# FFN first gemm of a transformer block: high and low activation halves as one 512-column operand, four products accumulating in one pair of banks

## Chip, cores and metric

The kernel runs on one core of one Trainium2 chip. The metric is the device time of one execution in microseconds, the median over several runs. A profile comes from one further execution under the hardware profiler.

## What is computed

One block: an attention and retention mixer with a residual, then a gated FFN with a residual, then a final norm. The change lies in the FFN and in the last lines of the final norm.

```python
S, D, D_FF = 512, 1024, 2816
hffn = modulate(rmsnorm(x, g_norm2[l]), shift2, scale2)
a, u = jnp.split(jnp.einsum('bsd,df->bsf', hffn, w_ffn_in[l]), 2, axis=-1)
x = x + gate2[:, None, :] * jnp.einsum('bsf,fd->bsd', jax.nn.silu(a) * u, w_ffn_out[l])
return rmsnorm(x, g_final)
```

Everything is float32.

## The kernel before

**Precision.** A float32 matmul is made of three matmuls in a faster 32-bit format (fp32r). Each operand is split into a high part, a rounded copy that ScalarE writes, and a low part, source minus high, that VectorE subtracts; high·high, high·low and low·high are accumulated. In names, whi and wlo are the two halves of a weight tile, and q, qp, v, s and h are pools whose tiles hold activations, weights or their halves.

**First gemm of the FFN.** The output columns of w_ffn_in are worked off in 11 pairs p (0 to 10): 256 columns of a and the 256 of u that belong to them. The tokens are two halves of 256 columns, and so is the contraction, two halves of 512 rows (four steps k of 128). The 2 × 2 × 2 block product is done with seven products instead of eight, on sums of blocks. The table SEVEN names the activation block of each: products 1 to 7 use A11, A12, S4, A22, S1, S2 and S3, where the S blocks are sums of the A blocks, made once. The weight blocks are summed for each pair on VectorE (`sums`, L1213). One product (`product`) is 2 column blocks of 128 × 4 steps k × 3 matmuls, each with 256 token columns: 24 matmuls into one PSUM bank, the two column blocks side by side in its 512 columns.

**What a product's result goes through** (`take_out`). Product 1 is copied out to p1; 2 goes on accumulating in the same bank and silu of the sum is s0; 6 is added to p1, giving u2; 5 is copied to c22; 7 is added to u2, and so on, until the pair's two results are split into high and low halves for the second gemm. Products 5, 6 and 7 each take a bank of the pool z, 1 and 4 one of the pool ps; 2 and 3 go on in the banks of 1 and 5.

**Second gemm.** Pairs are grouped in chunks (FF_CHUNKS: pair 0, then 1 and 2, 3 and 4, and so on). For each chunk there are four items ("out", c, i) of two output blocks each (`run_out`): 12 matmuls of 512 columns per block and 24 per item for a chunk of two pairs, half of that for chunk 0 with its one pair, then `residual` (L1158) on VectorE.

**Order.** The list `work` has all products and out items in the order in which they run; a pair's products go 1, 6, 5, 7, 2, 4, 3, with an out item after the third and the sixth. Weights are prepared AHEAD = 5 items ahead (`prepare_item`), and a scheduler then settles how the instructions of each engine are ordered. The FFN's opening, with all of pair 0 and parts of pairs 1 and 2, is written out by hand for PE, VectorE and ScalarE. Weight loads go out on SP's queue into the buffers raw (3) and araw (2). For products 1 and 2 the low half of the weights is not subtracted on VectorE: ScalarE writes the negative high half (L839), and a DMA of POOL's queue adds the raw weights to it (L840, `low_dma`). A pair's second such weight is named h<-raw in the trace, the first s<-raw.

**Tail.** The last blocks of the second gemm are done by halves of the tokens, squares are summed over the features by matmuls with ones, the roots taken (L1580 to L1584), and the rows multiplied and stored: `norm` (L1589, stores of `o`) for the first half of the tokens, `norm2` (L1603, stores of `fin`) for the second.

Of the kernel before, what the change touches and what calls it, by code (L numbers as in the profile page):

```python
# [19 lines left out]
P = 128  # L20
D = 1024
S = 512
# [93 lines left out]
def kernel(  # L116
# [1059 lines left out]
    def low7(key, src, tag):  # L1176
        hi, lo = acts7[key], quarter(tag)
        ins = nc.vector.tensor_sub(lo, src, f(hi))
        acts7[key] = tiles(hi), tiles(lo)
        return ins.ins  # L1180

# [67 lines left out]
    def product(p, n, o, first, last, at=None, then=None, late=None):  # L1249


        hi, lo = (tiles(t) for t in ready.pop((p, n)))
        ah, al = acts7[SEVEN[n]]
        early = ((hi, ah), (lo, ah)) if late == "a" else ((hi, ah), (hi, al))
        rest = (hi, al) if late == "a" else (lo, ah)
        for i in range(2):
            c = slice(i * P, (i + 1) * P)
            for k in range(4):
                if i * 4 + k == at:
                    then()  # L1260
                oc = o[:, i * 256 : (i + 1) * 256]
                a, z = first and i == 0 and k == 0, last and i == 1 and k == 3
                if late:
                    for n_, (w, x) in enumerate(early):
                        mm(oc, w[:, k, c], x[:, k, :], a and n_ == 0, False)
                else:
                    mm3(oc, hi[:, k, c], lo[:, k, c], ah[:, k, :], al[:, k, :], a, z)
        if late:
            w, x = rest
            for i in range(2):  # L1270
                c = slice(i * P, (i + 1) * P)
                for k in range(4):
                    ins = mm(o[:, i * 256 : (i + 1) * 256], w[:, k, c], x[:, k, :],
                             False, last and i == 1 and k == 3)
            return ins

    def run_product(p, n):

        d = part.setdefault(p, {})
        if n in (1, 4):  # L1280
            d["xy"[n > 1]] = ps()
        elif n in (5, 6, 7):
            d[" vzw"[n - 4]] = psz()
        product(p, n, d[" xxvyvzw"[n]], n not in (2, 3), n not in (1, 5))
        take_out(p, n)

    def take_out(p, n):
# [13 lines left out]
        elif n == 7:  # L1301
            d["u3"] = tmp()
            nc.vector.tensor_add(d["u3"], d["w"], d["u2"])
            nc.vector.tensor_add(d["c22"], d["c22"], d["u3"])
        elif n == 4:
            nc.vector.tensor_add(d["u3"], d["y"], d["u3"])
            nc.scalar.activation(d["u3"], d["u3"], AF.Silu)
        elif n == 3:
            tag = "h" if chunk_of[p] % 2 else "s"
            nc.vector.tensor_add(d["u2"], d["v"], d["u2"])  # L1310
            nc.vector.tensor_mul(d["u2"], d["u2"], d["s0"])
            nc.vector.tensor_mul(d["u3"], d["u3"], d["c22"])
            hi, lo = pair(tag), pair(tag)
            for hv, t in zip(HALVES, (d["u2"], d["u3"])):
                split(hi[:, :, hv], lo[:, :, hv], t.rearrange("p (a b) -> p a b", a=2))
            ff_acts[chunk_of[p]] += [(hi[:, i, :], lo[:, i, :]) for i in range(2)]
            del part[p]

# [70 lines left out]
    with tc.manual_schedule(engines={nc.vector.engine, nc.scalar.engine, nc.tensor.engine}):  # L1389
# [18 lines left out]
        for d in tail:  # L1408
# [16 lines left out]
        sq5 = square(5, h1)  # L1425
        high7("A11", m00, "v")
        scaled(m01, 1, range(2), h0, r0)
        add_square(sq5, h1)
        low7("A11", m00, "v")
# [4 lines left out]
        high7("A12", m01, "v")  # L1434
# [4 lines left out]
        a01, l01 = acts7["A12"], quarter("v")  # L1439
        nc.vector.tensor_sub(l01[:, 0:S], m01[:, 0:S], f(a01)[:, 0:S])  # L1440
        add_square(sq7, h1)
        acts7["A12"] = tiles(a01), tiles(l01)
        d0, d1 = part.setdefault(0, {}), part.setdefault(1, {})
# [6 lines left out]
        g1 = half_scale(  # L1450
            c1[0], lambda: nc.vector.tensor_sub(l01[:, S:], m01[:, S:], f(a01)[:, S:])
        )
# [8 lines left out]
        scaled(m11, 1, range(4), h1, r1[0])  # L1461
        high7("A22", m11, "q")
        scaled(m10, 0, range(4), h1, r1[0])
        ready[0, 5] = low(t0[5], k5, wtile("h"))
        low7("A22", m11, "q")
        d0["s0"] = tmp()
# [5 lines left out]
        nc.vector.tensor_sub(s2, s1, m00)  # L1472
        high7("S2", s2, "qp")
        nc.vector.tensor_sub(s4, m01, s2)
        low7("S2", s2, "q")
        product(1, 1, d1["x"], True, True)
# [6 lines left out]
        product(0, 6, d0["z"], True, True, late="a")  # L1483
        high7("S1", s1, "qp")
        ready[2, 1] = low_dma(raws_of[2][0, 0], k1, wtile("s"))
        nc.vector.tensor_sub(s3, m00, s3)
        low7("S1", s1, "q")
        high7("S3", s3, "q")
        ready[0, 7] = low(t0[7], k7, wtile("h"))
        low7("S3", s3, "q")  # L1490
# [4 lines left out]
        high7("S4", s4, "q")  # L1495
        prepare(2, 2)
# [3 lines left out]
        product(0, 7, d0["w"], True, True, late="a")  # L1500
        low7("S4", s4, "q")
        sums(1, t6="s")
# [57 lines left out]
    with tc.manual_schedule(engines={nc.vector.engine, nc.scalar.engine, nc.tensor.engine}):  # L1560
# [156 lines left out]
```

## Time and profile before

| | |
|---|---|
| runs, median | 1122.17 us (3 runs, 1121.74 to 1123.64) |
| profiled execution | 1121.0 us |
| its span | 1119.3 us, mean granted TensorE clock 0.997 |
| FFN with full engines | about 740 to 1105 us of the span |
| one pair of the FFN in its steady part | 31.08 us (896.00 to 927.08 between the same product of two pairs) |
| DMA over the span | 190.91 MB, mean 171 GB/s |

How rows read: a group of instructions has its line, engine, operation, out<-in by the program's names, tile shapes and count; then busy time in us, mean ns of one; then the idle time of the engine just before them and what ended it. "PE z L228 x24" in the chain is 24 matmuls into a bank of the pool z, each issued by the function at line 228. A chain's or timeline's row begins with its start in us and its length. A DMA row has its queue (SPq, POOLq), count, size, and us from issue to landing. The matmul's line is that of a helper, so its groups are told apart by names and shapes.

### The profile page before, as it was taken

Reading aid. Unit: us, or ns where it says so; the run is one execution under the profiler, and the core shown is the slowest. Engines: PE = TensorE matmul, PEld = TensorE weight load, DVE = VectorE, ACT = ScalarE, POOL = GpSimd, SP = SyncE. Lnnn points to the kernel's source line nnn. Section 1 sums busy time; section 2 is a strip of 40 time slices with the busy share of each in tenths; the row PEclk is TensorE's granted clock in tenths of the full one; section 3 lists DMA queues with packets and bytes.
Section 4 is the critical chain, followed back from the end, with each engine's and each line's share of the span. In section 5 each row is a group of like instructions: output and inputs, shape, how many; then the busy total and the mean of one; then the engine's idle time right before and its main releaser. Section 6 shows DMA issues by size and latency. Waiting matters only on the chain.

```text
span 1119.3 us, 15918 instructions
## 1 busy us (share of the span) xinstructions
PE 1105.4 (99%) x6096; PEld 961.4 (86%) x6096; DVE 836.9 (75%) x1174; ACT 553.7 (49%) x863; POOL 50.8 (5%) x78
## 2 busy tenths in 40 slices
PE   8999999999999999999999999999999999999996
PEld 6888888888888888888888888899999999999986
DVE  7899756959968958387788757568996677766656
ACT  5445345445444645355656654348654444544433
POOL 0000000010021020000000000000000000000000
PEclk9999999999999999999999999999999999999998
DMA  9714432766686476876676459462656555464322
GB/s 357 303 57 151 143 120 78 226 132 215 235 169 212 147 160 234 218 198 182 183 207 168 156 180 319 169 169 60 170 186 161 160 170 129 140 183 122 106 76 76
DMA packets 63148, 190.91 MB, mean 171 GB/s; under 512 B 7776, under 2 KB 9824, under 8 KB 63072
## 3 DMA queue, kind: packets, MB, share of 16 engines
q1 hardware_dynamic: 55760, 171.02, 47.0%
q0 software_dynamic: 6768, 18.35, 9.8%
q8 instruction: 48, 0.79, 0.3%
q10 hardware_dynamic: 544, 0.52, 0.1%
q14 instruction: 28, 0.23, 0.1%
HBM read 146.35 MB, written 16.78 MB: 146 GB/s over the span
## 4 chain that ended last, share of the span: by engine, by line
PE 93%; DVE 4%; issue 1%; DMA 1%; SPq 0%; ACT 0%; DVEq 0%; ACTq 0%
PE ps L228 70%; PE z L228 17%; PE av L228 3%; PE ps L636 1%; DVE s L870 1%; DVE wlo L208 1%; DMA sraw<-wada 1%; PE z L762 1%; DVE t L758 0%; PE av L636 0%; SPq L180 0%; DVE t L1033 0%; DVE q L881 0%; DVE s L209 0%; DVE fin L1603 0%
## 5 line engine op out<-in xcount | busy, mean ns | idle before, releaser
L228 PE MATMUL ps<-h,whi 128*128 128x512 f32 (+1 forms) x1154 | 334.3, 374 | 0.0
L228 PEld LDWEIGHTS ps<-h,whi 128*128 128x128 f32 x1154 | 208.8, 189 | 36.3 <-issue 0.5
L228 PE MATMUL ps<-h,wlo 128*128 128x512 f32 (+1 forms) x577 | 212.9, 372 | 0.0
L206 ACT ACTIVATE whi<-raw 128x1024 fp32r<-128x1024 f32 (+1 forms) x104 | 108.5, 1044 | 209.5 <-PE ps L228 161.7
L208 DVE TENSOR_TENSOR wlo<-raw,whi 128x1024 fp32r<-128x1024 f32 (+1 forms) x104 | 124.8, 1200 | 68.8 <-ACT whi L206 67.7
L228 PE MATMUL ps<-s,whi 128*128 128x512 f32 x480 | 148.5, 390 | 0.0
L228 PEld LDWEIGHTS ps<-h,wlo 128*128 128x128 f32 x577 | 108.7, 188 | 19.1
L228 PE MATMUL z<-q,whi 128*128 128x256 f32 x504 | 106.8, 283 | 0.0
L228 PEld LDWEIGHTS ps<-s,whi 128*128 128x128 f32 x480 | 89.3, 188 | 18.2 <-DVE s L208 0.3
L851 DVE TENSOR_TENSOR wlo<-s,whi 128x1024 fp32r<-128x1024 f32 x46 | 56.1, 1221 | 56.6 <-ACT whi L847 56.5
L228 PE MATMUL ps<-s,wlo 128*128 128x512 f32 x240 | 93.4, 389 | 0.0
L228 PEld LDWEIGHTS z<-q,whi 128*128 128x128 f32 x504 | 84.9, 192 | 1.5
L847 ACT ACTIVATE whi<-s 128x1024 fp32r<-128x1024 f32 x47 | 49.7, 1057 | 56.7 <-PE ps L228 45.7
L228 PE MATMUL ps<-whi,h 128*128 128x512 f32 x222 | 71.6, 391 | 0.0
L1158 DVE SCALAR_TENSOR_TENSOR o<-ps,mod,o 128x512 f32<-128x512 f32 (+1 forms) x63 | 42.4, 679 | 30.9 <-PE ps L228 30.9
L228 PEld LDWEIGHTS ps<-s,wlo 128*128 128x128 f32 x240 | 45.0, 188 | 9.4
L847 ACT ACTIVATE whi<-raw 128x1024 fp32r<-128x1024 f32 x28 | 29.6, 1058 | 43.1 <-PE ps L228 41.3
L228 PEld LDWEIGHTS ps<-whi,h 128*128 128x128 f32 x222 | 41.7, 188 | 9.5 <-ACT t L991 0.6
L228 PE MATMUL ps<-q,whi 128*128 128x256 f32 (+1 forms) x224 | 48.9, 313 | 0.0
L228 PE MATMUL z<-qp,whi 128*128 128x256 f32 x168 | 47.2, 283 | 0.0
L228 PE MATMUL z<-q,wlo 128*128 128x256 f32 x168 | 46.4, 283 | 0.0
L228 PE MATMUL z<-qp,wlo 128*128 128x256 f32 x160 | 45.3, 283 | 0.0
(324 smaller groups left out, 2096.3 us busy)
## 6 DMA issues: line engine op xcount, KB each, us to landing
raw<-wp SPq DMA_DIRECT2D x145, 512.0 KB, 4.1
araw<-wada SPq DMA_DIRECT2D x32, 512.0 KB, 4.0
araw<-wp SPq DMA_DIRECT2D x30, 512.0 KB, 5.4
s<-wp SPq DMA_DIRECT2D x24, 512.0 KB, 5.8
sraw<-wada SPq DMA_DIRECT2D x16, 512.0 KB, 8.5
q<-qp SPq DMA_DIRECT2D x32, 256.0 KB, 4.4
spill<-o POOLq DMA_DIRECT2D x24, 256.0 KB, 4.9
o<-xT SPq DMA_DIRECT2D x16, 256.0 KB, 4.3
```

What stands on the lines that cost most here:

```text
L206: nc.scalar.activation(dst_hi, src, AF.Copy, scale=scale)
L208: return (eng or nc.vector).tensor_sub(dst_lo, src, f(dst_hi))
L228: return nc.tensor.matmul(o, lhs, rhs, start=start, stop=stop, skip_group_check=True).ins
L636: nc.tensor.transpose(at[bank][:, c : c + P], t[:, a + j * P : a + (j + 1) * P], ident)
L762: nc.tensor.transpose(o[:, b * P : (b + 1) * P], sg[:, e * P : (e + 1) * P], ident)
L847: nc.scalar.activation(hi, t, AF.Copy)
L851: nc.vector.tensor_sub(lo, t, f(hi))
L870: nc.vector.tensor_tensor(dst[:, d], *((y, x) if swap else (x, y)), op=op)
L1158: return nc.vector.scalar_tensor_tensor(x1[d][:, hv], o[:, hv], mod[:, gcol + d : gcol + d + 1], x1[d][:, hv], op0=ALU.mult, op1=ALU.add,)
```

## The change

The activation tiles of the first gemm are laid out anew: for each k, 256 columns of the high part and 256 of the low part stand side by side, so that they can be read as one operand of 512 columns. From pair 2 on (WIDE = 2; pair 2's products 1 and 2 still run in the old form in the opening) a product is done by `wide_product`: for each of two banks and each k one matmul of the high weights with both halves (512 columns) and one of the low weights with the high half (256 columns, added to the right half of the bank). So a product has two banks, one for each column block, and each bank holds two halves whose sum is the result. Products 1, 6, 7 and 4 accumulate one after the other in one pair of ps banks, and after each the sum so far is read; 5 and 3 accumulate in the other pair, 2 has a pair of z banks. The order in a pair becomes 1, 5, out, 6, 2, 7, 3, 4, out. Reading is a ScalarE copy of one half and a VectorE addition of the other for each bank (`both_sums`), or two additions to an earlier sum (`both_added`). The second gemm's items take their banks from the pools z and av. In the tail the matmul `keep_busy` is dropped, and the last `norm` goes ahead of the roots.

```diff
-    def high7(key, src, tag):
-        acts7[key] = quarter(tag)
-        return nc.scalar.activation(acts7[key], src, AF.Copy).ins
+    def high7(key, src, tags):
+        acts7[key] = two = [quarter(t) for t in tags]
+        for n, t in enumerate(two):
+            ins = nc.scalar.activation(
+                parted(t)[:, :, 0, :], src[:, n * S : n * S + S].rearrange("p (k c) -> p k c", k=2), AF.Copy
+            )
+    def act7(key, k):
+        t = acts7[key][k // 2]
+        c = k % 2 * S
+        return t[:, c : c + 256], t[:, c + 256 : c + S], t[:, c : c + S]
...
-        if p > 1 and n == 6:
+        if p > 1 and n == (5 if p >= WIDE else 6):
             sums(p, t5="s", t6="s")
...
+    def wide_product(p, n, banks, first, last):
+        hi, lo = (tiles(t) for t in ready.pop((p, n)))
+        for i, o in enumerate(banks):
+            c = slice(i * P, (i + 1) * P)
+            for k in range(4):
+                ah, _, both = act7(SEVEN[n], k)
+                mm(o, hi[:, k, c], both, first and k == 0, False)
+                mm(o[:, 256:S], lo[:, k, c], ah, False, last and k == 3)
+
+    def both_sums(banks, t=None):
+        t = t or tmp()
+        for i, o in enumerate(banks):
+            c = t[:, i * 256 : i * 256 + 256]
+            nc.scalar.activation(c, o[:, 0:256], AF.Copy)
+            nc.vector.tensor_add(c, c, o[:, 256:S])
+        return t
+
+    def both_added(t, banks, u=None):
+        u = u or t
+        for part_ in (0, 256):
+            for i, o in enumerate(banks):
+                c = slice(i * 256, i * 256 + 256)
+                nc.vector.tensor_add(u[:, c], (t if part_ == 0 else u)[:, c], o[:, part_ : part_ + 256])
+        return u
+
+    def run_wide(p, n):
+        d = part.setdefault(p, {})
+        alone = "s0" in d
+        if n == (6 if alone else 1):
+            d["z"] = [ps(), ps()]
+        elif n == 5:
+            d["v"] = [ps(), ps()]
+        elif n == 2:
+            d["y"] = [psz(), psz()]
+        banks = d["v" if n in (3, 5) else "y" if n == 2 else "z"]
+        wide_product(p, n, banks, n in (1, 5, 2) or alone and n == 6, n in (2, 3, 4))
+        added = (lambda b: both_added(d["p1"], b, tmp())) if alone else both_sums
+        if n == 1:
+            d["p1"] = both_sums(banks)
+        elif n == 5:
+            d["p5"] = both_sums(banks)
+        elif n == 6:
+            d["u2"] = added(banks)
+        elif n == 2:
+            s0 = both_added(d["p1"], banks)
+            nc.scalar.activation(s0, s0, AF.Silu)
+        elif n == 7:
+            u3 = added(banks)
+            nc.vector.tensor_add(d["p5"], d["p5"], u3)
+        elif n == 3:
+            both_added(d["u2"], banks)
+            nc.vector.tensor_mul(d["u2"], d["u2"], d["s0" if alone else "p1"])
+        elif n == 4:
+            c21 = added(banks)
+            nc.scalar.activation(c21, c21, AF.Silu)
+            nc.vector.tensor_mul(c21, c21, d["p5"])
+            store_act(p, d["u2"], c21)
...
-            o = ps()
+            o = psa() if j else psz()
             gemm(o, w, ff_acts[c])
...
-            for n_, m in enumerate((1, 6, 5, 7, 2, 4, 3)):
+            wide = p >= 2
+            for n_, m in enumerate((1, 6, 5, 2, 7, 3, 4) if p == 1 == WIDE else (1, 5, 6, 2, 7, 3, 4) if wide else (1, 6, 5, 7, 2, 4, 3)):
                 if (p, m) not in FIRST:
                     work.append((p, m))
-                    if n_ in (2, 5) and len(outs) > (1 if c == NC - 1 else 0):
+                    if n_ in ((1, 6) if wide else (2, 5)) and len(outs) > (1 if c == NC - 1 else 0):
...
         mm(s1, ones, sqs[6], False, False)
-        keep_busy(1, ps())
         mm(s1, ones, sqs[7], False, True)
-        norm(range(2, 7))
+        norm(range(2, 8))
         roots(s1, r[:, h1])
         for n in range(4):
             norm2(n)
-        norm(range(7, 8))
```

How rows are ordered at three places, engine by engine. PE in pair 4, first before: the end of product 1 (operand s, bank ps) and the start of product 6 (bank z).

```order
L228 MATMUL ps_8038<-v_6764,s_7854 128x256
L228 MATMUL ps_8038<-v_6771,s_7854 128x256
L228 MATMUL ps_8038<-v_6764,s_7855 128x256
L228 MATMUL z_8069<-qp_6958,whi_7895 128x256
L228 MATMUL z_8069<-q_6961,whi_7895 128x256
L228 MATMUL z_8069<-qp_6958,wlo_7897 128x256
```

In the changed kernel, the end of the out item (bank av) ahead of pair 4 and the first step of product 1 (v is the activation tile, s the weights).

```order
L228 MATMUL av_7974<-h_7679,wlo_7803 128x512
L228 MATMUL av_7974<-h_7679,whi_7802 128x512
L228 MATMUL av_7974<-h_7680,whi_7802 128x512
L228 MATMUL av_7974<-h_7679,wlo_7803 128x512
L228 MATMUL ps_7994<-v_6764,s_7829 128x512
L228 MATMUL ps_7994<-v_6764,s_7830 128x256
```

Three matmuls of 256 columns for each step have become one of 512 and one of 256, and one activation tile (v_6764) is read where there were two (v_6764 and v_6771).

ScalarE (ACT) in pair 4, before: from the copy that takes product 1 out of its bank (L1291) to the negative of the next pair's second weight (h_8342 and h_8343). L1300 takes out product 5; the other rows split weights.

```order
L1291 ACTIVATE t_8063<-ps_8038 128x512
L839 ACTIVATE s_8166<-s_8165 128x1024
L847 ACTIVATE whi_8065<-h_8036 128x1024
L206 ACTIVATE whi_8098<-raw_8096 128x1024
L1300 ACTIVATE t_8127<-z_8102 128x512
L847 ACTIVATE whi_8131<-raw_8129 128x1024
L847 ACTIVATE h_8342<-raw_8340 128x1024
L847 ACTIVATE whi_8206<-s_8204 128x1024
L839 ACTIVATE h_8343<-h_8342 128x1024
```

In the changed kernel: ps_7994 and ps_7995 are the two banks that products 1, 6, 7 and 4 share. L1299 reads product 6 (the first two), then 7, then 4; h_8231 is the second weight of the next pair.

```order
L1299 ACTIVATE t_8100<-ps_7994 128x256
L206 ACTIVATE whi_8080<-raw_8078 128x1024
L1299 ACTIVATE t_8100<-ps_7995 128x256
L847 ACTIVATE h_8231<-raw_8229 128x1024
L839 ACTIVATE h_8232<-h_8231 128x1024
L1331 ACTIVATE t_8012<-t_8012 128x512
L1299 ACTIVATE t_8163<-ps_7994 128x256
L847 ACTIVATE whi_8143<-s_8139 128x1024
L1299 ACTIVATE t_8163<-ps_7995 128x256
L206 ACTIVATE whi_8171<-raw_8169 128x1024
L1299 ACTIVATE t_8216<-ps_7994 128x256
```

The copy of the next pair's second weight and its negative now stand between the reads of one bank after product 6 and after product 7.

VectorE (DVE) in pair 2, before: from a sum of weight blocks for pair 3 (s_7592) to the addition of product 4 (L1306), with that of product 7 (L1303) between.

```order
L1213 TENSOR_TENSOR s_7592<-araw_7572,s_7590 128x1024
L1303 TENSOR_TENSOR t_7623<-z_7598,t_7528 128x512
L1213 TENSOR_TENSOR h_7679<-araw_7572,araw_7570 128x1024
L851 TENSOR_TENSOR wlo_7596<-s_7592,whi_7594 128x1024
L1304 TENSOR_TENSOR t_7561<-t_7561,t_7623 128x512
L851 TENSOR_TENSOR wlo_7628<-s_7590,whi_7626 128x1024
L1306 TENSOR_TENSOR t_7623<-ps_7630,t_7623 128x512
```

In the changed kernel: the additions of product 6 (ps_7572 and ps_7573 into t_7590), of product 3's first bank (ps_7516), and of product 7 (into t_7619); the weight operations are for pair 3.

```order
L1308 TENSOR_TENSOR t_7590<-t_7204,ps_7572 128x256
L1308 TENSOR_TENSOR t_7590<-t_7204,ps_7573 128x256
L1308 TENSOR_TENSOR t_7590<-t_7590,ps_7572 128x256
L1308 TENSOR_TENSOR t_7590<-t_7590,ps_7573 128x256
L1222 TENSOR_TENSOR s_7595<-araw_7568,raw_7561 128x1024
L1308 TENSOR_TENSOR t_7590<-t_7590,ps_7516 128x256
L1222 TENSOR_TENSOR s_7597<-araw_7570,s_7595 128x1024
L851 TENSOR_TENSOR wlo_7601<-s_7595,whi_7599 128x1024
L1308 TENSOR_TENSOR t_7619<-t_7204,ps_7572 128x256
L1308 TENSOR_TENSOR t_7619<-t_7204,ps_7573 128x256
L1308 TENSOR_TENSOR t_7619<-t_7619,ps_7572 128x256
L1308 TENSOR_TENSOR t_7619<-t_7619,ps_7573 128x256
```

One addition per product has become four, and two sums of weight blocks and a subtraction stand between the additions that read the shared banks after product 6 and after product 7. In this pair product 3 comes between 6 and 7, and most of an out item between 7 and 4.

More of the change, by code (lines that the diff above doesn't have):

```diff
@@ L1170, with parted, low7 @@
     acts7 = {}
-    def high7(key, src, tag):
-        acts7[key] = quarter(tag)
-        return nc.scalar.activation(acts7[key], src, AF.Copy).ins
[L1176 to L1179, printed above, removed]
-        return ins.ins
+    def parted(t):
+        return t.rearrange("p (k h c) -> p k h c", k=2, h=2)
+    def high7(key, src, tags):
[4 more added lines that the diff above has]
+            )
+        return ins.ins
+    def low7(key, src, halves=(0, 1)):
+        for n in halves:
+            t = parted(acts7[key][n])
+            ins = nc.vector.tensor_sub(
+                t[:, :, 1, :], src[:, n * S : n * S + S].rearrange("p (k c) -> p k c", k=2), f(t[:, :, 0, :])
+            )
+        return ins.ins
+    def act7(key, k):
+        t = acts7[key][k // 2]
+        c = k % 2 * S
+        return t[:, c : c + 256], t[:, c + 256 : c + S], t[:, c : c + S]
     ready = {}
@@ L1252, in product @@
         hi, lo = (tiles(t) for t in ready.pop((p, n)))
-        ah, al = acts7[SEVEN[n]]
+        ah, al, _ = zip(*(act7(SEVEN[n], k) for k in range(4)))
         early = ((hi, ah), (lo, ah)) if late == "a" else ((hi, ah), (hi, al))
@@ L1264, in product @@
                     for n_, (w, x) in enumerate(early):
-                        mm(oc, w[:, k, c], x[:, k, :], a and n_ == 0, False)
+                        mm(oc, w[:, k, c], x[k], a and n_ == 0, False)
                 else:
-                    mm3(oc, hi[:, k, c], lo[:, k, c], ah[:, k, :], al[:, k, :], a, z)
+                    mm3(oc, hi[:, k, c], lo[:, k, c], ah[k], al[k], a, z)
         if late:
@@ L1277, in run_product, with store_act @@
+    def store_act(p, *halves):
+        tag = "h" if chunk_of[p] % 2 else "s"
+        hi, lo = pair(tag), pair(tag)
+        for hv, t in zip(HALVES, halves):
+            split(hi[:, :, hv], lo[:, :, hv], t.rearrange("p (a b) -> p a b", a=2))
+        ff_acts[chunk_of[p]] += [(hi[:, i, :], lo[:, i, :]) for i in range(2)]
+        del part[p]
+    WIDE = 2
     def run_product(p, n):
+        if p >= WIDE:
+            return run_wide(p, n)
         d = part.setdefault(p, {})
@@ L1312, in take_out @@
             nc.vector.tensor_mul(d["u3"], d["u3"], d["c22"])
[L1313 to L1317, printed above, removed]
+            store_act(p, d["u2"], d["u3"])
     def out_weight(c, i):
@@ L1438 @@
         sq7 = square(7, h1)
-        a01, l01 = acts7["A12"], quarter("v")
-        nc.vector.tensor_sub(l01[:, 0:S], m01[:, 0:S], f(a01)[:, 0:S])
+        low7("A12", m01, (0,))
         add_square(sq7, h1)
-        acts7["A12"] = tiles(a01), tiles(l01)
         d0, d1 = part.setdefault(0, {}), part.setdefault(1, {})
@@ L1450 @@
         g1 = half_scale(
[L1451 removed]
+            c1[0], lambda: low7("A12", m01, (1,))
         )
@@ L1472 @@
         nc.vector.tensor_sub(s2, s1, m00)
-        high7("S2", s2, "qp")
+        high7("S2", s2, ("qp", "q"))
         nc.vector.tensor_sub(s4, m01, s2)
-        low7("S2", s2, "q")
+        low7("S2", s2)
         product(1, 1, d1["x"], True, True)
```

25 lines of the change are left out of this document (12 added, 13 removed).

## The prediction

> **What bounds the kernel now.** I read the busy table first, then the chain of waits, then the windows of the FFN.
>
> ```profile
> span 1119.3 us, 15918 instructions
> PE 1105.4 (99%) x6096; PEld 961.4 (86%) x6096; DVE 836.9 (75%) x1174; ACT 553.7 (49%) x863; POOL 50.8 (5%) x78
> PE 93%; DVE 4%; issue 1%; DMA 1%; SPq 0%; ACT 0%; DVEq 0%; ACTq 0%
> ```
>
> TensorE is busy 99% of the span and holds 93% of the chain that ended last. In the stage that the change touches it has no gap at all:
>
> ```profile
> 800.00:833.00 33.00, 33.00 (x237) 31.16 (x236) 32.30 (x39) 15.91 (x19) 0.86 (x1) 1.00 0.52 152
> 900.00:940.00 40.00, 40.00 (x286) 37.82 (x285) 28.96 (x34) 18.50 (x23) 1.72 (x2) 1.00 0.46 132
> ```
>
> These are windows of PE, PEld, DVE, ACT, POOL, granted clock and DMA. PE fills both windows at clock 1.00. VectorE fills 72% of the later one (28.96 of 40), but 98% of the earlier one (32.30 of 33), the end of the FFN's opening. So a shorter matmul stream is a shorter kernel, as long as nothing else makes PE wait. The chain inside one weight pair gives the price of a matmul:
>
> ```profile
> 896.00 2.87 PE z L228 x24
> 901.75 5.76 PE z L228 x48
> 907.51 5.47 PE ps L228 x24
> ```
>
> A product is 24 matmuls of 256 columns: 2.87 us, 0.120 each. Half a second-gemm item is 12 matmuls, a whole one 24 of 512 columns: 5.47 us, 0.228 each. Twice the columns cost 1.90 times, so each matmul carries about 0.012 us that does not depend on its columns (2 × 0.120 − 0.228).
>
> **The change part by part.**
>
> *Wider operand.* A wide product has 8 matmuls of 512 and 8 of 256 instead of 24 of 256: 8 × 0.228 + 8 × 0.120 = 2.78 us against 2.87, so 0.093 us less. Pairs 3 to 10 have seven wide products and pair 2 has five, so 61 of them: −5.7 us. Every one lies on the bounding engine. There is still one weight load for each matmul, and the loads that are now in front of 512 columns have more cover than before, so I count nothing for loads. The bounds of this term are 0 (a wide matmul costs two narrow ones exactly) and −5.7.
>
> The Trainium skill, "VectorE: DVE Perf Modes", section "The TRN2 errata — SBUF-src ops pay a fixed extra latency per instruction", gives a matmul 6 cycles beside its columns at 2.4 GHz, 2.5 ns where the rows above give 12 ns; by it 61 × 8 × 2.5 ns, an estimate of 1.2 us, would be all that this part saves. The trace disagrees with it on the fixed part, and I go by the trace.
>
> *Evictions.* Halves that are added after the matmul cost more instructions: 18 VectorE operations of 256 columns and three of 512 in place of seven of 512, and ten ScalarE copies of 256 and two silus in place of four operations of 512.
>
> ```profile
> L1310 DVE TENSOR_TENSOR t<-z,t 128x512 f32<-128x512 f32 x7 | 4.8, 686 | 2.3 <-PE z L228 2.3
> L1405 DVE TENSOR_TENSOR s<-o,z 128x256 f32<-128x256 f32 x8 | 2.9, 414 | 0.6 <-PE z L228 0.6
> 769.63 2.74 DVE L1405 TENSOR_TENSOR h<-o,z 128x256 f32<-128x256 f32 x8 [0.59 <-PE z L228]
> L206 ACT ACTIVATE s<-av 128x256 fp32r<-128x256 f32 x16 | 6.3, 394 | 0.0
> L1307 ACT ACTIVATE t<-t 128x512 f32<-128x512 f32 x7 | 4.3, 618 | 1.3 <-DVE t L1306 1.3
> ```
>
> The first row is the 512-column add, the second the 256-column one, and the third shows eight of these back to back in 2.74 us, 0.34 each: successive operations overlap by 0.07. With 0.61 for a 512-column one that is 18 × 0.34 + 3 × 0.61 − 7 × 0.61 = 3.7 us more VectorE work per pair of about 31 us, 72% becoming some 84%; ScalarE goes from 46% to about 55%. Neither becomes the bound; TensorE's own work covers it, and I count nothing, except where the cover fails in the two parts that follow. Without cover it would be 3.7 us × 8 pairs.
>
> *The shared banks.* Products 1, 6, 7 and 4 now accumulate in one pair of banks, and each partial sum must be read before the next product may add to it. Before, each had a bank to itself. Between 6 and 7 lies product 2, between 7 and 4 product 3: 2.78 us of cover, 4.17 for each bank (the next product comes to the second bank 1.39 us after the first). A read is a ScalarE copy of 0.39 and a VectorE add of 0.41; even with a 1.06 us weight copy and a 1.22 us weight subtraction queued between them it is 3.1 us, and it fits. It does not fit in two places.
>
> The Trainium skill, "Perfetto Trace Analysis", section "Matmuls", advises that independent groups rotate through banks so that reading one overlaps the next; this change gives that up for four products of seven. The row of L1310 above waits only for PE, and no run so far shows the reverse wait; the two prices below are worked out without this rule.
>
> *Place one, pair 2.* There VectorE comes out of the opening without idle (the window 800 to 833 above). From reading product 6 to reading product 7 its queue holds, as the excerpt in the section on the change shows, 8 adds of 0.34, one more of 0.34, two weight sums and one weight subtraction of about 1.14: 6.5 us. TensorE needs 2 × 2.78 + 12 × 0.228 = 8.3 us from the end of product 6 to the start of product 4 (products 3 and 7 and an out item of chunk 0). So 1.8 us of lag are covered; the work added per pair (3.7) is the most that a queue without idle is late by: a stall of 0 to 1.9, and product 5 of pair 3, queued behind, can add as much again. I take 1.65, bounds 0 and 3.7.
>
> *Place two, pairs 4 and 7.* In ScalarE's queue the copy of the next pair's second weights (h<-raw at L847 and its negative, L839) now stands between the reads of product 6 and product 7. Its data is late for a reason that the transfers show:
>
> ```profile
> raw<-wp SPq DMA_DIRECT2D x32, 512.0 KB, 4.1
> h<-raw POOLq DMA_DIRECT2D x7, 512.0 KB, 4.6
> s<-raw POOLq DMA_DIRECT2D x6, 512.0 KB, 7.6
> 906.27 1.64 SPq L1196 DMA_DIRECT2D araw<-wp  x2
> 907.77 0.87 POOL L840 DMA_DIRECT2D s<-raw  x1 [12.59 <-DVE s L1213]
> 915.64 0.33 SPq L201 DMA_DIRECT2D raw<-wp  x1
> L847 ACT ACTIVATE h<-raw 128x1024 fp32r<-128x1024 f32 x7 | 7.4, 1056 | 24.7 <-DMA raw<-wp 24.7
> ACT h L847 <- DMA raw<-wp: 24.7, 4, 8.3
> ```
>
> (Transfers of 860 to 1060 with issue to landing; three issues in order of time; the copy's group; its waits: total, times, longest.) The accumulating transfer s<-raw reads a buffer, and the next raw load goes into that buffer, so it starts only when the transfer is through: issued at 907.77, next raw at 915.64. ScalarE waits up to 8.3 us for that load already; harmless until now, since nothing behind it was urgent. In the changed order, with T the start of product 1, the transfer is issued after the first half of product 5 is read: 4.17 + 0.39 + 3 × 1.055 + 0.39 + 1.055 = T + 9.2. With d for its length, the load lands 4.1 later, two copies (2.1), a silu (0.62) and the read (0.39) follow on ScalarE, then on VectorE an add (0.41), two operations of 1.22 and the last add (0.41): T + 19.7 + d, some 0.4 less for overlaps. The second bank is needed at T + 22.1 + 1.39 = 23.5. Stall: d − 4.2 for each of the two pairs.
>
> What is d? 4.6 where nothing runs beside (h<-raw), 7.6 where the two araw loads run beside (s<-raw, as at 906.27). In the changed order the araw loads are through before the transfer, and one raw load is under way, for part of it: one of two gives half of the 3.0, half covered gives a quarter, d = 5.3. So 2 × (5.3 − 4.2) = +2.2. What is queued behind the waiting copy is the reads of products 7 and 4, and product 4 waits for them. In the other pairs the copy stands elsewhere, except in pair 8, where it costs up to 2.1 with d = 7.6 and nothing at 5.3.
>
> *High and low halves* are written in two instructions of 512 instead of one of 1024: 2 × 0.61 against 1.14 on VectorE, seven times, 0.6 us in the opening; hidden by TensorE's stream there, part of the lag at pair 2 otherwise.
>
> *The second gemm's banks* (psz and psa in place of ps): its evictions (0.75 each) are 5.5 us ahead of the bank's next use; nothing.
>
> *The tail.*
>
> ```profile
> 1109.03 0.70 PE L228 MATMUL z<-t,ones 128*128 128x256 f32 x2 [0.27 <-ACT t L1568]
> 1109.37 0.57 PE L228 MATMUL ps<-negones 128*128 128x512 f32 x1
> 1114.06 1.58 ACTq L1606 DMA_DIRECT2D out_dram<-fin  x2
> 1115.15 0.48 DVE L1589 SCALAR_TENSOR_TENSOR o<-o,gfh,t 128x256 f32<-128x256 f32 x1
> 1115.66 0.34 SPq L1592 DMA_DIRECT2D out_dram<-o  x1
> ```
>
> A 512-column matmul (0.22 in its pitch) leaves the last chain, and the last store, issued at 1115.66, goes out earlier, so that fin's second one of 1114.06 + 1.58 ends the kernel: 0.36 earlier at the last issue, and part of the 0.22 is lost because VectorE now has the moved operation ahead of the roots. −0.4, bounds 0 and −0.6.
>
> **Sum.** −5.7 − 0.4 + 1.65 + 2.2 = −2.25 us. The profiled execution took 1121.0 us, its span 1119.3 and 1.7 around it; the sum gives 1118.75 for such an execution. The runs' median, 1122.17, is 1.2 above that, and a measured median would be 1119.9.
>
> **Rivals.**
>
> *No stall but a trifle.* The transfer takes 4.6 and VectorE is in time at pair 2: −6.1 + 0.8 = −5.3, 1116.9. For it: seven of thirteen transfers do take 4.6. Against it: VectorE's 98% before pair 2.
>
> *The transfer is the bound: slower.* If the pair 4 and 7 transfers still meet two loads, d is 7.6: 2 × 3.4 + 2.1 (pair 8) + 1.65 − 6.1 = +4.45, 1126.6. It decides from d = 6.4 on, where the two stalls (4.4) and pair 2 eat the whole saving. For it: 7.6 is the median of the window's six s<-raw. Against: in the changed order the loads come earlier than the transfer.
>
> *A wide matmul saves nothing.* If 512 columns beside 256 on one operand cost as much as three narrow ones, the sum is −0.4 + 1.65 + 2.2 = +3.45, 1125.6. For it: only that no product mixes both widths in the trace. Against: the pitch of 0.228 in rows of the same stage, with the same loads. With the skill's 2.5 ns the sum would be 1124.4, on this side too.
>
> **How the numbers follow.** Forecast 0.42, own range 1117.5 to 1122 (d from 4.6 to 6, pair 2 from 0 to 3.7); no stall 0.24; transfer 0.24; no saving 0.10. A change of 0.2% is 2.24 us, about what can be told from none. Faster by more: all of the second and half of the first, 0.45. Slower by more: the last two and 0.03 of the first, 0.37. Within: 0.18. The range reaches from 1116, below the case without stalls, to 1127.5, above the case of the transfer: it leaves out about 0.1 on each side, for stalls in more pairs than two and for a tail that gains its most.
>
> **What would show it.** Wide products take 2.78 us each in the chain; if they take 2.87, the first term is wrong. PE shows idle in the FFN, where it had none, ahead of product 4 in pairs 2, 4 and 7, released by VectorE's adds; its sum beside 3.9 us decides between the cases. The s<-raw transfers show 5 to 6 us; 7 or more means the slower case. If PE waits in every pair, the cover of 2.78 us was mis-sized, and all of it is wrong. The last thing to land is a store of fin.

## The result, and the profile after

The changed kernel takes 1128.88 us (median of 5 runs, 1126.61 to 1134.42) against 1122.17 (also 5 runs, 1121.74 to 1123.64): a ratio of 1.0063, 95% interval 1.0033 to 1.0092. It is slower by 6.7 us; the forecast was 1119.9, the range ended at 1127.5, and the rival that came nearest was the late transfer (1126.6). The execution profiled here is the slowest of the five, 1134.42 us; a second profile stands among the experiments.

Page of the changed kernel, busy times and the engines' shares of the chain that ended last:

```profile
span 1132.7 us, 15139 instructions
PE 1109.7 (98%) x5607; PEld 938.8 (83%) x5607; DVE 868.0 (77%) x1306; ACT 571.7 (50%) x935; POOL 49.9 (4%) x78
PE 79%; DVE 10%; DMA 6%; issue 3%; ACT 2%; SPq 0%; DVEq 0%; ACTq 0%; POOLq 0%
```

TensorE's share of the chain fell from 93% to 79%: DMA, VectorE and ScalarE are now steps of it. PE's busy time did not fall although 489 matmuls are gone. What the chain looks like in a pair that runs undisturbed (pair 5), and what came ahead of it in pair 4:

```profile
884.15 2.83 PE ps L228 x16
887.01 0.64 DVE s L1222
...
890.52 3.60 DMA raw<-wp
894.23 1.07 ACT h L847
...
896.28 0.61 ACT t L1331
897.67 4.76 PE ps L228 x16
...
907.88 5.64 PE ps L228 x32
...
918.98 2.81 PE ps L228 x16
921.79 2.83 PE z L228 x16
```

The last three rows are wide products: 2.81 to 2.83 us each, 5.64 for two, where 2.78 was forecast and 2.87 stood before. The row of 4.76 is pair 4's product 4, 16 matmuls in 1.7 times the length, and ahead of it the chain goes through a raw load and ScalarE. ScalarE's own timeline there shows the queue that the prediction described:

```profile
886.89 1.06 ACT L206 ACTIVATE whi<-raw 128x1024 fp32r<-128x1024 f32 x1 [0.91 <-PE ps L228]
887.85 0.37 ACT L1299 ACTIVATE t<-ps 128x256 f32<-128x256 f32 x1
894.23 1.06 ACT L847 ACTIVATE h<-raw 128x1024 fp32r<-128x1024 f32 x1 [6.01 <-DMA raw<-wp]
895.32 1.06 ACT L839 ACTIVATE h<-h 128x1024 fp32r<-128x1024 f32 x1
896.28 0.61 ACT L1331 ACTIVATE t<-t 128x512 f32<-128x512 f32 x1
896.80 0.36 ACT L1299 ACTIVATE t<-ps 128x256 f32<-128x256 f32 x1
```

L1299 at 887.85 reads product 6, L1299 at 896.80 reads product 7, and between them ScalarE stood 6.01 us before the copy of the next pair's second weight. SP's and POOL's issues, and the transfer's length, say why the load was late:

```profile
883.77 0.33 SPq L201 DMA_DIRECT2D raw<-wp  x1
890.52 0.80 SPq L1205 DMA_DIRECT2D raw<-wp  x2
```

```profile
883.80 0.86 POOL L840 DMA_DIRECT2D s<-raw  x1 [15.08 <-ACT s L839]
```

```profile
s<-raw POOLq DMA_DIRECT2D x1, 512.0 KB, 6.7
```

The accumulating transfer went out at 883.80, together with a raw load of 883.77, and took 6.7 us; 883.80 + 6.7 = 890.5, the very time at which the next raw load was issued. By the formula of the prediction the stall is 6.7 − 4.2 = 2.5 us. TensorE's timeline has 2.23 us of waiting at that place (2.4 from matmul to matmul):

```profile
897.67 0.61 PE L228 MATMUL ps<-q,whi 128*128 128x512 f32 x1 [2.23 <-DVE t L1300]
```

Windows around the two places at which TensorE stopped (PE, PEld, DVE, ACT, POOL, granted clock, DMA share, GB/s) show a loss of which the prediction had no term:

```profile
895.00:897.00 2.00, 0.45 (x3) 0.13 (x2) 0.37 (x1) 1.97 (x4) 0.33 (x1) 1.00 0.00 0
897.00:900.00 3.00, 2.33 (x8) 1.94 (x8) 2.81 (x4) 2.33 (x4) 0.52 (x1) 0.65 0.69 131
900.00:903.00 3.00, 3.00 (x14) 2.37 (x13) 3.00 (x7) 1.04 (x2) 0.00 (x0) 0.78 0.92 240
1017.00:1020.00 3.00, 0.72 (x5) 0.35 (x3) 0.42 (x1) 1.82 (x3) 0.00 (x0) 1.00 0.17 68
1020.00:1023.00 3.00, 2.29 (x8) 1.60 (x8) 1.57 (x3) 2.05 (x4) 0.85 (x1) 0.63 0.34 66
1023.00:1026.00 3.00, 2.96 (x9) 2.57 (x10) 3.00 (x7) 0.84 (x2) 0.00 (x0) 0.50 1.00 214
1026.00:1029.00 3.00, 3.00 (x14) 2.52 (x14) 3.00 (x5) 1.12 (x2) 0.00 (x0) 0.73 0.86 262
```

After the idle TensorE works, but at a granted clock of 0.50 to 0.78 on the mean of these windows. In the trace's clock records it is 0.5 from 897.91 to 901.32 and from 1020.79 to 1027.61. In 1023 to 1026 it is busy for 2.96 us and does 9 matmuls; at full clock, 0.177 on the mean of a wide product's 16, it would have done 17. The second place is pair 8, ahead of product 7. There ScalarE's copy of the next pair's second weight waits for its load as well, and the read of product 6 stands behind it:

```profile
1018.18 1.06 ACT L847 ACTIVATE h<-raw 128x1024 fp32r<-128x1024 f32 x1 [5.22 <-DMA raw<-wp]
1019.14 0.36 ACT L1299 ACTIVATE t<-ps 128x256 f32<-128x256 f32 x1
```

The account of this execution, from starts of matmuls against their pitch at full clock: pair 4 lost 4.2 us (2.4 idle), pair 7 1.0, pair 8 6.2 (3.5 idle): 11.4. The wide products saved 61 × 0.05 = 3.1 and the tail 0.5 (last work of the kernel: from the start of fin at L1676 to the end of the span 6.22 us, before 6.56; and 0.16 ahead of that). That is +7.8. The span grew by 13.4; the other 5.6 lie in front of the FFN, in code that the change does not touch (counted directly, by the start of pair 0's product 6, it is 5.9).

### The profile page after: what moved, and what is told of

It is laid out like the page before. It is cut to its first block, busy times and chain, and to the rows that moved or that the text cites. A ratio compares the mean times of both kernels' runs of the same rounds, so it can differ in the third digit from the quotient of the medians.

```text
span 1132.7 us, 15139 instructions
## 1 busy us (share of the span) xinstructions
PE 1109.7 (98%) x5607; PEld 938.8 (83%) x5607; DVE 868.0 (77%) x1306; ACT 571.7 (50%) x935; POOL 49.9 (4%) x78
## 4 chain that ended last, share of the span: by engine, by line
PE 79%; DVE 10%; DMA 6%; issue 3%; ACT 2%; SPq 0%; DVEq 0%; ACTq 0%; POOLq 0%
PE ps L228 60%; PE z L228 11%; PE av L228 6%; DMA araw<-wada 2%; DMA raw<-wp 2%; DVE araw L256 1%; DVE wlo L851 1%; PE ps L636 1%; DVE s L870 1%; DVE wlo L208 1%; DMA s<-raw 1%; DMA sraw<-wada 1%; DVE t L758 0%; PE z L762 0%; DMA h<-raw 0%
## 5 line engine op out<-in xcount | busy, mean ns | idle before, releaser
L228 PE MATMUL ps<-h,whi 128*128 128x512 f32 (+1 forms) x1026 | 294.8, 372 | 0.0
L228 PE MATMUL ps<-q,whi 128*128 128x512 f32 (+1 forms) x368 | 131.1, 402 | 5.8 <-DVE t L1300 5.7
L228 PE MATMUL ps<-s,whi 128*128 128x512 f32 x320 | 98.9, 390 | 0.3 <-DVE s L208 0.3
L228 PE MATMUL ps<-q,wlo 128*128 128x256 f32 (+1 forms) x328 | 97.4, 297 | 0.0
L228 PEld LDWEIGHTS ps<-q,whi 128*128 128x128 f32 x368 | 70.5, 193 | 24.3 <-DVE t L1300 8.1
L228 PEld LDWEIGHTS ps<-q,wlo 128*128 128x128 f32 x328 | 63.9, 195 | 1.3
L228 PE MATMUL ps<-s,wlo 128*128 128x512 f32 x160 | 62.2, 389 | 0.0
L256 DVE SCALAR_TENSOR_TENSOR araw<-araw,cact 128x1024 f32<-128x1024 f32 x32 | 39.1, 1228 | 8.4 <-DMA araw<-wada 8.3
L851 DVE TENSOR_TENSOR wlo<-raw,whi 128x1024 fp32r<-128x1024 f32 x26 | 31.8, 1223 | 16.7 <-ACT whi L847 16.7
L228 PE MATMUL ps<-wlo,h 128*128 128x512 f32 x111 | 43.2, 390 | 0.0
L1299 ACT ACTIVATE t<-ps 128x256 f32<-128x256 f32 x82 | 30.1, 372 | 23.1 <-PE ps L228 23.0
```

Source lines behind the costliest of these rows:

```text
L228: return nc.tensor.matmul(o, lhs, rhs, start=start, stop=stop, skip_group_check=True).ins
L256: nc.vector.scalar_tensor_tensor(raw, raw, 1.0, cact, op0=ALU.mult, op1=ALU.mult, accum_out=col)
L851: nc.vector.tensor_sub(lo, t, f(hi))
L1299: nc.scalar.activation(c, o[:, 0:256], AF.Copy)
```

## The experiments

Four questions: does the stall come again; is the late buffer its cause; what does the mixed width cost; and does idle time itself lower the clock.

**The changed kernel again.**

> The changed kernel once more, for a second profile. Theory: the FFN holds TensorE idle of about 2.4 us ahead of product 4 of pair 4 and of product 7 of pair 8 and about 2 and 4 us more at half the granted clock behind them; these stand in any execution, and the median is again 1127 to 1130. Rival: the time lies in front of the FFN, where the first profile was 5.8 us behind the kernel before in code that did not change; then those 5.8 us come again, and the FFN's waits vary.

Measured: 1129.87 us (1127.64 to 1132.99; before 1122.44), ratio 1.0077 (1.0059 to 1.0095); the span of the profile 1125.9. Windows of this profile:

```profile
891.00:894.00 3.00, 0.97 (x6) 0.70 (x5) 1.27 (x2) 3.00 (x6) 0.85 (x1) 1.00 0.16 31
894.00:897.00 3.00, 2.08 (x13) 1.57 (x12) 3.00 (x7) 1.25 (x2) 0.00 (x0) 1.00 0.99 213
1012.00:1015.00 3.00, 0.88 (x6) 0.51 (x4) 0.28 (x1) 1.64 (x3) 0.00 (x0) 1.00 0.18 74
1015.00:1018.00 3.00, 2.78 (x8) 1.98 (x8) 1.53 (x3) 1.85 (x3) 0.85 (x1) 0.56 0.26 49
```

The same two places stop again, 2.19 us ahead of pair 4's product 4 (and 1.08 ahead of its second bank) and 2.47 ahead of pair 8's product 7. The clock fell behind the second and stayed at 1.00 behind the first, so that is not the same in every execution. Of the loss in front of the FFN 1.4 us came again. The theory holds for the place; the account closes: some 9 us of idle and low clock, 3.6 saved, 1.4 in front, +6.8 by this sum, and the span is 6.6 longer than before. The execution profiled is the fastest of this kernel's four here.

**The buffer freed early.** From pair 4 on the low half of product 1's weights is subtracted on VectorE:

```diff
-            w = split_dma(raws_of[p][n - 1, 0], *(wtile(t) for t in tags or " sh"[n] * 2))
+            if n == 1 and p > 3:
+                raw = raws_of[p][0, 0]
+                w = low(raw, high(raw, wtile("s")), wtile("s"))
+            else:
+                w = split_dma(raws_of[p][n - 1, 0], *(wtile(t) for t in tags or " sh"[n] * 2))
```

> The change, but from pair 4 on the low half of product 1's weights is subtracted on VectorE instead of being accumulated by POOL's transfer, so that the raw buffer is free early. Theory (the transfer holds the buffer that the next pair's second weight is loaded into): no raw load is late, the idle ahead of product 4 (pair 4) and product 7 (pair 8) goes, and with it the low clock: 12 us less than the changed kernel's profile, 1117 to 1120. Rival (VectorE is too full to read the shared banks in time): it gets 1.2 us more work per pair, the idle stays or grows, 1129 to 1133.

Measured: 1120.43 us (1118.62 to 1124.02), 0.9984 of before (0.9973 to 0.9995): 8.5 and 9.4 us under the changed kernel's two medians and 0.4 above the expected range, with more work on VectorE. The stops in pairs 4, 7 and 8 are gone. TensorE's waits in the FFN in this run, as total, times and longest:

```profile
PE ps L228 <- DVE t L1304: 1.4, 1, 1.4
PE ps L228 <- DVE t L1312: 0.7, 1, 0.7
```

They lie elsewhere: 1.54 us at 865, pair 3, and 0.89 at 831, pair 2. The late transfer is the cause of the large loss; the rival, too little VectorE time, is at most true of the small rest. The edit takes away the transfer and ScalarE's negation along with the hold on the buffer; that it is the buffer which counts is seen from when the load goes out, in the next run.

**The same from pair 5 on** (`p > 4` in place of `p > 3`).

> The change with product 1's low half subtracted on VectorE from pair 5 on, and the matmul order of the change. Theory: pairs 4 and 8 lose their idle as in the run with the same edit from pair 4 on, and the 1.54 us at 865 do not come: 1118 to 1120. Against the run with both edits it shows what the order of the matmuls is worth without any idle: 61 x 0.03 = 1.5 to 2 us. Rival: the idle at 865 comes again, then it is not the subtraction that made it.

Measured: 1120.17 us (1119.01 to 1121.78; before 1123.27 in that comparison), 0.9975 (0.9966 to 0.9984), 0.2 above the expected range. Windows, then the copy in ScalarE's timeline and the load's issue:

```profile
860.00:900.00 40.00, 40.00 (x207) 33.89 (x207) 36.54 (x57) 22.89 (x34) 1.72 (x2) 1.00 0.64 187
1000.00:1060.00 60.00, 60.00 (x315) 51.17 (x315) 48.81 (x76) 29.68 (x46) 1.72 (x2) 1.00 0.40 121
```

```profile
886.70 1.06 ACT L847 ACTIVATE h<-raw 128x1024 fp32r<-128x1024 f32 x1 [1.78 <-DMA raw<-wp]
```

```profile
882.88 4.72 SPq L1205 DMA_DIRECT2D raw<-wp  x2
```

PE fills both windows that held the stops, at clock 1.00. The raw load goes out at 882.88 instead of 890.52, which is 4.3 us earlier counted from the start of product 1, and ScalarE waits 1.78 us instead of 6.01. The idle at 865 does not come: it was the earlier subtraction that made it.

**The order of widths.** In each bank the four matmuls of 512 columns first, then the four of 256:

```diff
             for k in range(4):
-                ah, _, both = act7(SEVEN[n], k)
-                mm(o, hi[:, k, c], both, first and k == 0, False)
-                mm(o[:, 256:S], lo[:, k, c], ah, False, last and k == 3)
+                mm(o, hi[:, k, c], act7(SEVEN[n], k)[2], first and k == 0, False)
+            for k in range(4):
+                mm(o[:, 256:S], lo[:, k, c], act7(SEVEN[n], k)[0], False, last and k == 3)
```

> The change, but in each bank the four 512-column matmuls come first and then the four of 256 columns. Theory (a pair of 512 and 256 takes 0.353 us, not 0.348, because the widths alternate and a 0.19 us weight load stands ahead of each narrow one): the product returns to 2.78 us or goes above 2.83 where the narrow ones follow each other. Rival (the two pitches add as 0.235 + 0.118 in any order): it stays at 2.82 to 2.83. In time within 2.5 us of the changed kernel in both cases.

Measured: 1125.4 us (1125.04 to 1126.44), 1.0029 (1.0017 to 1.0041). The chain of this run in pair 5, and the windows of pair 4's stop:

```profile
902.12 5.59 PE ps L228 x32
...
913.19 2.78 PE ps L228 x16
915.97 2.81 PE z L228 x16
```

```profile
891.00:894.00 3.00, 1.62 (x8) 1.28 (x8) 2.09 (x3) 3.00 (x6) 0.85 (x1) 1.00 0.27 53
894.00:897.00 3.00, 2.06 (x12) 1.76 (x12) 3.00 (x6) 1.62 (x3) 0.00 (x0) 1.00 1.00 197
```

Two products take 5.59 where they took 5.64, and one in the y banks 2.81 where it took 2.83: about 0.025 each. The halves of the out items that follow take up to 0.03 more, so that a whole pair gains 0.12 (30.57 us from one product 1 to the next, against 30.69), some 1.0 us in the FFN. So alternating widths is part of what the forecast of 2.78 missed, against the rival. The median is 4.5 us below the changed kernel's second, where at most 2.5 was expected. Of this the two profiles have 2.2: 1.0 from the order, 0.6 in front of the FFN, and 0.4 in idle and clock (8.6 us in all against 9.0). The idles are only spread otherwise, 1.9 and 1.1 in pair 4, 1.4 and 1.1 in pair 7 (more than there before) and 1.9 in pair 8, and the clock stays at 1.00 behind all of them. What makes up the rest between the medians is not shown.

**Idle by itself.** The kernel before, with VectorE copies of product 7's bank and a matmul that must wait for them:

```diff
+    GAPS = {3: 3, 5: 5, 7: 8, 9: 12}
...
         take_out(p, n)
+        if n == 7 and p in GAPS:
+            t = tmp()
+            for _ in range(GAPS[p]):
+                nc.vector.tensor_copy(t, d["w"])
+            keep_busy(1, d["w"])
```

> The kernel before, with TensorE held up in pairs 3, 5, 7 and 9: 3, 5, 8 and 12 extra VectorE copies read product 7's bank, and one extra 512-column matmul that writes this bank has to wait for them. Theory (idle of TensorE itself lowers its granted clock): behind each idle of 2 us or more some 4 to 8 us follow at half the clock, 2 to 4 us lost beside the idle; behind idle under 1 us nothing is lost. Rival (the clock falls because of something else in the changed kernel, wide matmuls for example): matmuls are back at 0.120 and 0.228 us right behind the idle.

Measured in one run: 1128.64 us, and a profile of span 1126.9. The scheduler moved the copies and the extra matmul apart, so only two of the four held TensorE up: 0.46 us at 858 in pair 3, and 3.82 us at 990 in pair 7. Windows of the second:

```profile
990.00:994.00 4.00, 0.51 (x5) 0.30 (x3) 4.00 (x6) 1.58 (x2) 0.00 (x0) 0.90 0.69 131
994.00:996.00 2.00, 1.84 (x7) 1.75 (x8) 2.00 (x4) 0.00 (x0) 0.00 (x0) 0.50 0.44 86
996.00:998.00 2.00, 2.00 (x12) 2.00 (x11) 0.50 (x1) 0.63 (x1) 0.00 (x0) 0.50 0.87 248
998.00:1000.00 2.00, 2.00 (x11) 2.00 (x11) 0.91 (x2) 1.06 (x1) 0.00 (x0) 0.50 0.52 199
1000.00:1002.00 2.00, 2.00 (x19) 2.00 (x17) 2.00 (x3) 1.50 (x2) 0.00 (x0) 0.99 0.00 0
```

In a kernel without any wide matmul 3.8 us of idle are followed by 6 us at 0.50: 2.7 us lost on top. Behind 0.46 us nothing happened. The rival, wide matmuls as the cause, falls, on one execution with one long idle.

**Both edits.** The subtraction from pair 5 on and the 512-column matmuls first.

> The change with both edits: product 1's low half subtracted on VectorE, now only from pair 5 on, and the 512-column matmuls first in each bank. Theory: pair 4 no longer pays the 1.54 us that the subtraction cost it at 865 in the last run, since that subtraction came with pair 4's own weights, and a product takes 2.79 instead of 2.82: no idle over 0.5 us ahead of products 4 and 7, some 3 us below the run with the first edit alone, 1116.5 to 1118.5. Rival (VectorE's load is what is late): idle of 1 to 2 us moves to another pair, 1119 to 1122.

Measured: 1119.86 us (1117.74 to 1122.58), 0.9975 (0.9965 to 0.9985), above the forecast: pair 8 stops for 0.51 and 1.52 us, pair 7 for 0.36, which gives back what the order gains. The time is the rival's, but its reason, VectorE's load, is not what the trace shows in pair 8:

```profile
1006.22 1.06 ACT L847 ACTIVATE h<-raw 128x1024 fp32r<-128x1024 f32 x1 [3.17 <-DMA raw<-wp]
1007.59 0.42 DVE L1304 TENSOR_TENSOR t<-t,ps 128x256 f32<-128x256 f32 x1 [2.14 <-ACT t L1303]
```

VectorE stands idle for 2.14 us, waiting for ScalarE, and ScalarE waits 3.17 for a raw load: a late load once more.

**More cover by the out items.** 512 first, and the second gemm's items where the shared banks are read:

```diff
-                    if n_ in ((1, 6) if wide else (2, 5)) and len(outs) > (1 if c == NC - 1 else 0):
+                    if n_ in ((3, 5) if wide else (2, 5)) and len(outs) > (1 if c == NC - 1 else 0):
```

> The change with the 512-column matmuls first and with the second gemm's items in the two places where the shared banks are read: 1, 5, 6, 2, out, 7, 3, out, 4. Theory (the raw load is late by a fixed time against a deadline): 5.5 us more cover before products 7 and 4 hold the late copy, and the idle there goes; new idle can arise ahead of product 6, whose only cover is product 5: 1117 to 1121. Rival (the order of ScalarE's queue moves along with the order of products, so that the copy is late by as much again): idle of 2 us stays, 1125 to 1127.

Measured: 1121.04 us (1119.05 to 1124.1), 0.9983 (0.9972 to 0.9994). The stops of pairs 4, 7 and 8 are gone, though POOL's transfer is still made. One of 1.46 us is new, in pair 2. VectorE's timeline there:

```profile
833.38 1.22 DVE L1222 TENSOR_TENSOR s<-araw,s 128x1024 f32<-128x1024 f32 x1
836.77 1.23 DVE L851 TENSOR_TENSOR wlo<-s,whi 128x1024 fp32r<-128x1024 f32 x1 [2.17 <-ACT whi L847]
837.91 1.08 DVE L1308 TENSOR_TENSOR t<-t,ps 128x256 f32<-128x256 f32 x3
```

This is the order in front of product 7's additions that the prediction feared for pair 2; here the weight subtraction waits 2.17 us and the additions behind it are late.

**The out items from pair 3 on**, pair 2 as in the change (`(3, 5) if p > 2 else (1, 6) if wide`), and the same with the subtraction of product 1's low half from pair 5 on.

> 512-column matmuls first, and the second gemm's items placed ahead of products 7 and 4 from pair 3 on; pair 2 keeps the change's order. Theory (in pair 2 the reads of product 7 wait behind a weight subtraction, and moving its item took the cover away): the 1.46 us at 837 of the earlier run goes and nothing else comes, 1.5 us less than that run, 1118.5 to 1120.5. Rival (VectorE is behind at the end of the opening whatever the order): 1 to 2 us stay near 835.

> The same with product 1's low half subtracted on VectorE from pair 5 on. Theory: with the longer cover the late buffer costs nothing any more, so that the two remedies do not add: within 0.7 us of the run with the same order alone, and above it if VectorE's 1.2 us per pair delay a read. Rival: raw loads were still late there, and 1 us or more is gained.

Measured: 1119.2 us (1117.97 to 1120.39), 0.9967 (0.9954 to 0.9979), and 1118.74 (1117.77 to 1119.39), 0.9964 (0.995 to 0.9978), before 1123.15 in both. TensorE waits for nothing in the FFN of either (740 to 1100 us), and in the first of the two POOL's transfer is still there. The remedies do not add: 0.46 us between them is within the spread, and from the start of the FFN to the end both profiles take the same time to 0.1 us. Either beats the kernel before by about 0.35%. The FFN windows of the last:

```profile
860.00:900.00 40.00, 40.00 (x209) 34.11 (x208) 36.82 (x57) 20.08 (x30) 0.86 (x1) 1.00 0.56 170
1000.00:1060.00 60.00, 60.00 (x316) 51.34 (x315) 50.38 (x77) 30.22 (x46) 1.72 (x2) 1.00 0.40 122
```

PE and clock are full, while VectorE does 92% and 84% of the windows: a load as high as this does not hold TensorE up.

**Nothing wide.** WIDE = 99, with the old order and banks, the new layout and the new tail.

> The changed kernel with no pair wide: the order and the banks of the kernel before, but the new layout of the activations in two instructions each and the new tail. Theory (layout costs nothing, the tail gives 0.4 to 0.5): 0.4 us below the kernel before, no verdict beyond 0.2%. Rival (the layout costs the full opening 1 to 2 us): 1 us or more above it.

Measured: 1121.68 us (1120.53 to 1124.8) against 1123.27, 0.9988 (0.9978 to 0.9999), and the profile's span is 1118.8 against 1119.3. The layout costs nothing; the tail gives the half microsecond, and the interval leaves room for more.

## Why the prediction was wrong

**The mechanism was named, its price was too small.** The prediction saw that the next pair's second weight would be copied between the reads of the shared banks, that its load waits for POOL's transfer, and that the stall is d − 4.2. The formula came near: d of 6.7 gives 2.5; 2.4 was measured in the first profile and 3.3 (2.19 and 1.08, one for each bank) in the second, where d was 6.6; in the first the low clock stretched the first half of product 4 and so probably hid the second bank's wait. That the formula came so near is in part luck: with the transfer's true start as well (1.55 later, see below) it gives about 4, so its other terms were too long. The step that failed first is "half covered gives a quarter, d = 5.3": the raw load goes out in the same 0.03 us as the transfer, so the cover is whole; 4.6 + 1.5 = 6.1 by the same reasoning, and 6.7 in the trace. The step before it was off too: the transfer went out 10.75 us after the start of product 1 (883.80 against 873.05), not 9.2, because ScalarE waited 1.6 us for the raw data of the first copy. Together they made 2.4 to 3.3 us of 1.1. Pair 7 was mis-sized the other way (d of 4.7; 0.84 us between matmuls against 1.1).

**Pair 8 was ruled out too early.** "Nothing at 5.3, up to 2.1 with d = 7.6": d was 6.2, with no load beside it, which no run here explains; the idle was 2.45 and 1.03 in the first profile and 2.47 in the second. There the copy stands in ScalarE's queue between the reads of product 5 and those of product 6, so that product 7, not 4, is the one that waits.

**No term for the clock.** The sum priced idle at its own length. Behind idle of 2.4 us and more TensorE got half its clock for 3.4 or 6.8 us: 1.8 and 2.7 us more in the first profile, where this is the largest single omission, and 1.5 in the second. The run with idle alone shows that the idle does it.

**The wide product** saves 0.05, not 0.093: 2.82, not 2.78. The direction was right; the error was to add two pitches taken from uniform streams. Ordering by width recovers 0.025. By the 2.5 ns that the prediction takes from the Trainium skill ("VectorE: DVE Perf Modes", "The TRN2 errata — SBUF-src ops pay a fixed extra latency per instruction") the saving would be 1.2 us in all, an estimate; measured are 3.1.

**Pair 2** cost nothing in the changed kernel where 1.65 was counted; the same order did cost 1.46 us when the out item behind it was moved. **VectorE and ScalarE** as engines were off the path, as counted. **The tail** gave 0.5, forecast 0.4. **The forecast of the likeliest case** erred mostly because three stops were priced at 2.2 us in all that cost 9 to 12 with the clock; the rival of the late transfer, at 6.8 + 2.1 for the same three stops, had a chance of 0.24 and lay 2.3 us under the result.

**Open.** In the wide kernels' profiles the time in front of the FFN is longer than in the three profiles of kernels with narrow products, and the prediction had no term for it: pair 0's product 6 starts at 779.2 to 779.5 us in the narrow ones and at 780.4 to 785.4 in the nine wide ones, though every engine runs the same instructions there. Of the first profile's 5.9 us some 2 are there by 40 us, where the clock was at 0.5 from 17.27 to 20.68; most of the rest comes where VectorE waits for loads (araw<-wada; longest 3.0 us). Why these come late was not tested. That all nine lie above all three points to the change. But two of the three narrow profiles (1121.0 and 1120.5 us) come from the fast end of executions that range from 1120.5 to 1125.5, so it may be chance of the executions as well; how much of the 6.7 us it is in the medians is not known. The median of before itself moved between 1122.2 and 1123.3 from one comparison to the next.

## What to carry to other kernels

Accumulating in shared banks turns every slow item in an eviction engine's queue into a deadline for TensorE, so ask first what in that queue waits for a transfer, and move it away from the reads or free its buffer early. Price a stop of a full TensorE at its length plus what the clock costs behind it. A wider operand saved 0.05 us a product where two uniform streams promise 0.093, so measure the mixed stream before counting on it.

## What the hardware showed

The granted clock behind an idle of TensorE in the FFN, with the idles measured from the starts of matmuls in seven profiles: those up to 2.19 us (0.46, 1.46, 1.52, 1.54, 1.87, 1.90 and 2.19 among them) cost nothing beyond themselves, 2.38, 2.45, 2.47 and 3.82 us brought it down to 0.5.

The length of the idle alone may not decide. Within one execution the clock records change only at times that lie a multiple of 3.41 us apart: in the first profile at 897.91, 901.32, 1020.79 and 1027.61 (1, 35 and 2 such steps), in the run with idle alone at 993.23 and 1000.06 (2 steps). Cut into such stretches, the four that end in a fall hold 2.4, 2.4, 2.5 and 2.9 us of idle, and no other in the FFN holds more than 1.9. The idle of 2.19 us lay across the border at 892.50 and put only 1.48 into one stretch and, with the 1.08 after it, 1.79 into the next. So in these runs the border lies between 1.9 and 2.4 us of idle in one stretch, and whether an idle near it lowers the clock can depend on where it falls. The low clock then lasted one stretch (3.4 us) or two (6.8), the second where a further 0.9 us or more of idle fell into the first. That cost 1.5 to 2.7 us each time.
